# VectorE and SyncE in program order, merged branches split during the last gate block, and the next input without GpSimd, in a two-layer hybrid backbone

## The chip, the cores and the metric

The kernel runs on one core of one Trainium2 chip. The metric is the time of one execution on the device, in microseconds (us); three executions of the kernel before took 2442.62, 2447.07 and 2448.18 us, median 2447.07.

## The reference

Two layers, 512 tokens (256 context, 256 latent), width 2048, everything in fp32. In short, for each layer:

```python
mod = silu(c) @ w_ada[l] + b_ada[l]            # shift, scale, gate; the same of c_ctx
h   = rms_norm(x, norm_g[l]) * (1 + scale) + shift
proj = h @ w_in[l]                             # 2048 -> 12288
y_f = (fourier_mix(f_x) * silu(f_g)) @ w_up_fourier
y_p = (pool_mix(p_x)    * silu(p_g)) @ w_up_pool
# retention, 8 heads of 128: q, k rotated by position (latent tokens only),
# scores with exponential decays in both directions, plus the state of the context
o   = head_rms(o_f + flip(o_b));  y_r = (o * silu(r_g)) @ w_up_ret
g   = sigmoid(proj[:, 6144:])                  # three gates of 2048
x   = x + gate * ((g0 * y_f + g1 * y_p + g2 * y_r) @ w_out)
# ctx gets the same in layer 0; in layer 1 the context gives only k and v
return rms_norm(x, final_norm_g)
```

## The kernel before, in words

**Weights.** Every weight matrix is streamed in chunks of 256 rows by 512 columns (`raw`, 512 KB, four buffers, loaded by SyncE, L196). An fp32 product is made of three products of a rounded high part and the rest, so each chunk is split: ScalarE copies it to the rounded high part `whi` (L206), VectorE subtracts that from `raw` and gives the low part `wlo` (L207). `whi` and `wlo` have three buffers each. TensorE then runs the chunk's products (`mm3`, L151 to L153: two matmuls with `whi`, one with `wlo`). `stream` (L241 to L264) walks over all 512 chunks: it splits the chunk two ahead, loads the one four ahead and runs the products of the present one. So `whi` of a chunk can be written only when TensorE has ended the chunk three before. A chunk is 24 or more products in layer 0 (512 tokens) and mostly 12 in layer 1 (256 tokens).

**Small work.** Between the products stand rotations, decays, scores, norms, transposes. They wait in a queue, `mix` (class Steps, L162 to L182): each entry has a `gap` in modelled microseconds, and `mix.passed` pops entries as products are emitted. A popped entry writes its instructions into the program at that place, for all engines it uses.

**Background.** Gates and modulations of the layers are matrix-vector products on VectorE: units of one `bgraw` load (512 KB, two buffers, on SyncE) and four products with `bga` (L466, L468). `stream` pops a unit behind five of every eight chunks.

**Order.** TensorE runs in the order in which the program text emits its instructions. In the kernel before, the instructions of VectorE, ScalarE, GpSimd and SyncE are put in order by a scheduler; TensorE's are not. Each engine runs its own list strictly in order, and an instruction that waits holds up all behind it.

**Names.** `rope_a` (GpSimd, L597) and `rope_b` (VectorE, L604, L605) rotate q and k; `heads_T` transposes them (L684). `decays_a` makes decay tables (VectorE L708, L709, then three exponentials on ScalarE L710 to L712), `decays_b` finishes them on GpSimd, `scores` multiplies q and k (L732) and weighs the result (VectorE L734), `attend` applies it (L744, L747), `squares` (GpSimd L754, then a split) and `norm_a` (a sum on TensorE L761, a root on ScalarE L762) and `norm_b` (VectorE reciprocal L766, product L767) are the head norm. The generic split of an activation is L431 (ScalarE, high part) and L432 (VectorE, low part). `gated` multiplies by SiLU (L614), SiLU itself is L572. `projected` (L1011 to L1022) adds the residual and, after a row's last piece, takes its sum, a root on ScalarE (L1021) and a reciprocal on VectorE (L1022). `scaled` (GpSimd, L1085) and `next_h` (ScalarE, L1092) make the next layer's input from the transposed rows.

## Time and profile before

| | |
|---|---|
| three executions | 2442.62, 2447.07, 2448.18 us |
| the profiled execution | 2445.55 us, span 2443.8 us |
| TensorE busy | 2392.4 us, 98% |
| VectorE busy | 1320.6 us, 54% |
| ScalarE busy | 870.4 us, 36% |
| GpSimd busy | 240.3 us, 10% |
| mean DMA rate | 162 GB/s |

TensorE is the engine that is nearly always busy, so what counts is where it is not, or where its clock is lower. A matmul's record ends later than the next begins, so busy time is a union of records. In the stretches below, PEclk is the granted clock as a share of 2.4 GHz; 0.5 is 1.2 GHz. Of an engine's idle time the trace names what ended it.

### The profile page before, as it was taken

How to read it: one execution, taken by the hardware profiler on the slowest of the kernel's cores; microseconds unless marked ns; L12 is line 12 of the kernel's file. 1: busy time of each engine (PE TensorE's matmuls, PEld its weight loads, DVE VectorE, ACT ScalarE, POOL GpSimd, SP SyncE). 2: the span in 40 equal slices, each digit the busy share in tenths (PEclk: the TensorE clock that was granted, in tenths of full speed). 3: DMA queues.
4: the chain of work that ended last, by engine and by line, in shares of the span. 5: the costliest groups of instructions: out<-in, count | busy, mean ns of one | idle time of the engine just before them, and what ended most of it. 6: DMA issues, size and time to landing. Idle time of an engine off the chain costs nothing.

```text
span 2443.8 us, 28705 instructions
## 1 busy us (share of the span) xinstructions
PE 2392.4 (98%) x11288; PEld 1967.8 (81%) x11288; DVE 1320.6 (54%) x1656; ACT 870.4 (36%) x1180; POOL 240.3 (10%) x246
## 2 busy tenths in 40 slices
PE   6999999999999999999999999999999999999998
PEld 3678788778888888888888888878889888888886
DVE  4437657768256258644457432653527544545555
ACT  5222332342222232222222322563426444444444
POOL 0000200200000001110011210230302000110100
PEclk9999999999999999999999999999999999999999
DMA  9955424346345336545466343443335666676664
GB/s 338 348 170 173 138 78 148 92 136 213 115 144 187 93 119 210 156 128 169 130 202 215 112 129 112 147 150 103 100 90 146 211 191 180 181 216 183 189 204 146
DMA packets 226471, 396.58 MB, mean 162 GB/s; under 512 B 14032, under 2 KB 55376, under 8 KB 226336
## 3 DMA queue, kind: packets, MB, share of 16 engines
q1 hardware_dynamic: 221088, 379.74, 50.8%
q0 software_dynamic: 5248, 15.01, 2.1%
q8 instruction: 88, 1.44, 0.2%
q14 instruction: 47, 0.39, 0.1%
HBM read 392.60 MB, written 2.10 MB: 162 GB/s over the span
## 4 chain that ended last, share of the span: by engine, by line
PE 81%; issue 8%; DMA 5%; DVE 4%; POOL 1%; ACT 1%; SPq 0%; DVEq 0%; POOLq 0%; ACTq 0%
PE acc L151 25%; PE acc L152 25%; PE acc L153 25%; DVE bga L468 2%; DMA wa<-in_w_ada_dram 2%; DMA bgraw<-in_w_ada_dram 1%; DVE wlo L207 1%; PE mx L323 1%; PE mx L744 1%; PE mx L732 1%; PE mx L747 1%; POOL g L1085 1%; PE mx L701 0%; DMA raw<-in_w_out_dram 0%; PE mx L889 0%
## 5 line engine op out<-in xcount | busy, mean ns | idle before, releaser
L207 DVE TENSOR_TENSOR wlo<-raw,whi 128x1024 fp32r<-128x1024 f32 (+1 forms) x504 | 624.6, 1240 | 824.5 <-ACT whi L206 824.0
L206 ACT ACTIVATE whi<-raw 128x1024 fp32r<-128x1024 f32 (+1 forms) x504 | 529.2, 1050 | 1153.4 <-PE acc L153 553.5
L151 PE MATMUL acc<-whi,hm 128*128 128x512 f32 x1568 | 621.9, 397 | 0.7 <-ACT g L577 0.7
L152 PE MATMUL acc<-wlo,hm 128*128 128x512 f32 x1568 | 611.7, 390 | 2.2 <-DVE wlo L207 2.2
L153 PE MATMUL acc<-whi,hm 128*128 128x512 f32 x1568 | 611.7, 390 | 0.0
L151 PE MATMUL acc<-hm,whi 128*128 128x512 f32 (+1 forms) x1232 | 461.1, 374 | 0.7 <-ACT whi L206 0.7
L153 PE MATMUL acc<-hm,wlo 128*128 128x512 f32 (+1 forms) x1232 | 453.0, 368 | 1.0 <-DVE wlo L207 1.0
L152 PE MATMUL acc<-hm,whi 128*128 128x512 f32 (+1 forms) x1232 | 452.7, 367 | 0.0
L152 PEld LDWEIGHTS acc<-wlo,hm 128*128 128x128 f32 x1568 | 295.1, 188 | 62.7 <-DVE wlo L207 4.1
L153 PEld LDWEIGHTS acc<-whi,hm 128*128 128x128 f32 x1568 | 294.7, 188 | 62.3
L151 PEld LDWEIGHTS acc<-whi,hm 128*128 128x128 f32 x1568 | 295.0, 188 | 61.2 <-ACT g L577 1.1
L468 DVE SCALAR_TENSOR_TENSOR bga<-bgraw,sc,bga 128x512 f32<-128x512 f32 x420 | 311.8, 789 | 53.1 <-DMA bgraw<-in_w_ada_dram 51.5
L151 PEld LDWEIGHTS acc<-hm,whi 128*128 128x128 f32 x1232 | 232.6, 189 | 42.4 <-ACT whi L206 2.2
L153 PEld LDWEIGHTS acc<-hm,wlo 128*128 128x128 f32 x1232 | 232.4, 189 | 40.5 <-DVE wlo L207 2.2
L152 PEld LDWEIGHTS acc<-hm,whi 128*128 128x128 f32 x1232 | 232.6, 189 | 39.4 <-issue 1.4
L852 POOL TENSOR_TENSOR g<-g,g 128x512 f32<-128x512 f32 x32 | 52.7, 1673 | 726.5 <-DVE g L848 726.5
L151 PE MATMUL acc<-g,whi 128*128 128x512 f32 x256 | 99.7, 390 | 0.0
L152 PE MATMUL acc<-g,whi 128*128 128x512 f32 x256 | 99.6, 389 | 0.0
L153 PE MATMUL acc<-g,wlo 128*128 128x512 f32 x256 | 99.6, 389 | 0.0
L597 POOL TENSOR_TENSOR g<-g,g 128x256 f32<-128x256 f32 x32 | 29.6, 954 | 332.4 <-ACT g L577 332.4
L151 PEld LDWEIGHTS acc<-g,whi 128*128 128x128 f32 x256 | 48.1, 188 | 10.1
L152 PEld LDWEIGHTS acc<-g,whi 128*128 128x128 f32 x256 | 48.1, 188 | 10.0
(213 smaller groups left out, 1888.4 us busy)
## 6 DMA issues: line engine op xcount, KB each, us to landing
raw<-in_w_in_dram SPq DMA_DIRECT2D x368, 512.0 KB, 3.7
bgraw<-in_w_ada_dram SPq DMA_DIRECT2D x128, 512.0 KB, 4.3
raw<-in_w_out_dram SPq DMA_DIRECT2D x72, 512.0 KB, 3.6
wa<-in_w_ada_dram SPq DMA_DIRECT2D x128, 256.0 KB, 6.0
raw<-in_w_up_ret_dram SPq DMA_DIRECT2D x32, 512.0 KB, 3.8
raw<-in_w_up_fourier_dram SPq DMA_DIRECT2D x16, 512.0 KB, 3.7
raw<-in_w_up_pool_dram SPq DMA_DIRECT2D x16, 512.0 KB, 4.4
w<-in_w_in_dram SPq DMA_DIRECT2D x8, 512.0 KB, 6.6
```

The source lines that it names most:

```text
L151: T.matmul(ps, ah, bh, start=first, stop=False)
L152: T.matmul(ps, ah, bl, start=False, stop=False)
L153: at["product"] = T.matmul(ps, al, bh, start=False, stop=last)
L206: S.activation(hi[:, :, 0:w], raw[:, :, 0:w], AF.Copy)
L207: V.tensor_tensor(lo[:, :, 0:w], raw[:, :, 0:w], hi[:, :, 0:w].bitcast(F32), op=ALU.subtract)
L323: T.matmul(ps[32 * g4:32 * g4 + 32, 0:2 * n * P], sc32[:, kt, :], wa[gi, kt // rows][:, kt % rows, :, :].rearrange("p i c -> p (i c)"), st ...
L468: V.scalar_tensor_tensor(accs[ci, v], raw[:, kk, :], s, accs[ci, v], op0=ALU.mult, op1=ALU.add)
L597: G.tensor_tensor(rv[:, :, :, x, :], pv[:, :, :, 1 - x, :], sv[:, :, x, :].unsqueeze(1).to_broadcast([P, 4, 2, 32]), op=ALU.mult)
L732: T.matmul(ps[:, jt * SEQ:(jt + 1) * SEQ], self.kT[hh][:, k0:k0 + P], qs, start=True, stop=True)
L744: T.matmul(o, self.v[2 * s + jt][:, c], at[:, jt * SEQ:(jt + 1) * SEQ], start=jt == 0, stop=jt == 1 and s == 0)
L747: T.matmul(o, self.st[d][:, c], qd[:, d * SEQ:(d + 1) * SEQ], start=False, stop=d == 1)
L852: G.tensor_tensor(merged[d][:, 0:ntok], merged[d][:, 0:ntok], o[:, 0:ntok], op=ALU.add)
```

## The change

1. `stream` of all blocks runs with VectorE and SyncE in the order of the program text too, from the first block to the end of the program. ScalarE and GpSimd are still put in order by the scheduler.
2. Chunks of blocks whose split weights are kept (the last block) are split one chunk earlier.
3. Background units are popped only when the queue `mix` has fewer than two entries, behind three of every four chunks.
4. The small work is queued in larger pieces with other gaps: transposes of two heads at once, both states at once, the scores of a head together with the product of the one before, windows and pooled pieces in pairs. In layer 1 k is transposed for its two latent tiles instead of all four.
5. The merged branches are split as they are finished in the last gate block, or in pairs just before the output projection needs them, instead of all sixteen at its start (layer 0); in layer 1 one entry transposes and splits a whole piece.
6. The next layer's input: the scaling moves from GpSimd to VectorE and takes the modulation with it; ScalarE adds the shift while rounding to the high part, VectorE subtracts for the low part.
7. Half of the last output DMAs are issued by ScalarE.

Line numbers shift: L432, L614, L766 become L434, L616, L766; L1020, L1022 become L1028, L1030; L572 becomes L574.

```diff
@@ -258,9 +258,11 @@
         yield
         for i in range(n):
             prepare(i + 2)
+            if i + 3 < n and chunks[i + 3][0].keep:
+                prepare(i + 3)
             ahead(i + 4)
             chunks[i][0].products(chunks[i][1], parts.pop(i))
-            if i > 5 and i % 8 in (1, 3, 5, 6, 7) and bg:
+            if i > 5 and len(mix.q) < 2 and i % 4 and bg:
                 bg.popleft()()
 
 
...
@@ -635,14 +637,14 @@
                 self.k[t] = evac(ps)
                 if t == 3:
                     for t2 in (2, 3):
-                        mix.append(lambda t2=t2: rope_a(self.k, t2), gap=0.8, after=2.0)
-                    mix.append(lambda: self.decayed(0), gap=1.6)
+                        mix.append(lambda t2=t2: rope_a(self.k, t2), gap=1.6, after=2.0)
+                    for d in range(2):
+                        mix.append(lambda d=d: self.decayed(d), gap=1.6)
                     for t2 in (2, 3):
                         mix.append(lambda t2=t2: rope_b(self.k, t2), gap=1.0)
-                    mix.append(lambda: (self.state(0), self.decayed(1)), gap=1.6)
-                    for hh in range(4):
-                        mix.append(lambda hh=hh: self.heads_T(self.k, (0, 1, 2, 3), self.kT, hh))
-                    mix.append(lambda: self.state(1))
+                    mix.append(lambda: (self.state(0), self.state(1)), gap=3.0)
+                    for hh in (0, 2):
+                        mix.append(lambda hh=hh: self.heads_T(self.k, tiles, self.kT, hh), gap=4.0)
                     if last:
                         self.queue_heads()
 
@@ -650,55 +652,53 @@
                 self.q[t] = evac(ps)
                 if t == 3:
                     for t2 in (2, 3):
-                        mix.append(lambda t2=t2: rope_a(self.q, t2), gap=1.2, after=2.0)
+                        mix.append(lambda t2=t2: rope_a(self.q, t2), gap=2.5, after=2.0)
                     for t2 in (2, 3):
                         mix.append(lambda t2=t2: rope_b(self.q, t2), gap=1.0)
-                    for hh in range(4):
-                        mix.append(lambda hh=hh: self.heads_T(self.q, tiles, self.qT, hh))
+                    for hh in (0, 2):
+                        mix.append(lambda hh=hh: self.heads_T(self.q, tiles, self.qT, hh), gap=4.0)
                     if not last:
                         self.queue_heads()
 
             def queue_heads(self):
                 for hh in range(4):
-                    mix.append(lambda hh=hh: self.decays_a(hh), gap=1.0)
+                    mix.append(lambda hh=hh: self.decays_a(hh), gap=2.0)
                 for hh in range(4):
                     mix.append(lambda hh=hh: self.decays_b(hh), gap=1.0)
                 for hh in range(5):
-                    if hh < 4:
-                        mix.append(lambda hh=hh: self.scores(hh))
-                    if hh:
-                        mix.append(lambda hh=hh: self.attend(hh - 1))
+                    mix.append(lambda hh=hh: (self.attend(hh - 1) if hh else None, self.scores(hh) if hh < 4 else None), gap=4.0)
                     if hh > 1:
                         mix.append(lambda hh=hh: self.squares(hh - 2), gap=1.0)
                 mix.append(lambda: self.squares(3), gap=1.0)
                 for hh in range(4):
                     mix.append(lambda hh=hh: self.norm_a(hh))
                 for hh in range(4):
-                    mix.append(lambda hh=hh: self.norm_b(hh))
-
-            def heads_T(self, src, tls, dst, hd):
+                    mix.append(lambda hh=hh: self.norm_b(hh), gap=2.0 if last else 5.0)
+
...
@@ -850,12 +852,24 @@
                         merged[d] = o
                     else:
                         G.tensor_tensor(merged[d][:, 0:ntok], merged[d][:, 0:ntok], o[:, 0:ntok], op=ALU.add)
+                    if final and j == 3:
+                        mix.append(lambda: split_merged(d), gap=0.8, after=0.5)
+
+                def up_before(j=j):
+                    if j == 0:
+                        mix.flush()
 
                 if j == 1 and b == 0:
                     start_at_block(lambda: [bg_gate(l, jj, seqs) for jj in range(4)])
                 fblock(C_MG + b * D + 512 * j, 4, gate_done)
+                if final and j == 3:
+
+                    blocks[-1].during = {k0: lambda d=k0 - 2: (split_merged(d), split_merged(d + 1)) for k0 in range(2, 14, 2)}
                 blocks.append(Block(wview(wname, l, 512 * j, 512), nkt, 512, [("F", i * P, 0, ntok) for i in range(4)],
-                                    lambda kt, t0, n: tuple(x[:, t0:t0 + n] for x in y[kt]), up_done, before=mix.flush if j == 0 else None))
...
@@ -916,10 +930,8 @@
             silu_f[i] = silu(ps)
             if i == 3:
                 for n in range(6):
-                    if n < 4:
-                        mix.append(lambda n=n: positions(n))
-                    if 1 <= n < 5:
-                        mix.append(lambda n=n: channels(n - 1))
+                    if n < 5:
+                        mix.append(lambda n=n: (channels(n - 1) if n else None, positions(n) if n < 4 else None), gap=4.0)
                     if n > 1:
                         mix.append(lambda n=n: mirrored(n - 2), gap=1.0)
...
@@ -993,16 +1004,13 @@
 
         sst, rs = {}, {}
 
-        def split_merged(d):
-            m[d] = split(merged.pop(d), ntok, hmt)
-
         def out_start():
             while bg:
                 bg.popleft()()
-            if not last:
-                mix.flush()
-                for d in range(KT):
-                    split_merged(d)
+
+        def merged_until(kt):
+            while kt not in m:
+                mix.q.popleft()[0]()
 
         def projected(j, t, ps, c0=0, n=512):
             xin = xins.pop((j, t)) if l == 0 else xres[t, j]
...
@@ -1082,15 +1092,18 @@
 
             def scaled(s, kt):
                 xt = xT[s, kt // 2][:, (kt % 2) * SEQ:(kt % 2 + 1) * SEQ]
-                G.tensor_tensor(xt, xt, xT[s][:, 0:SEQ], op=ALU.mult)
+                V.scalar_tensor_tensor(xt, xt, gs[1][:, kt, s:s + 1], xT[s][:, 0:SEQ], op0=ALU.mult, op1=ALU.mult)
                 return xt
 
             def next_h(s, kt):
                 if kt + 1 < KT:
                     xts[s, kt + 1] = scaled(s, kt + 1)
                 xt = xts.pop((s, kt))
-                S.activation(xt, xt, AF.Identity, scale=gs[1][:, kt, s:s + 1], bias=sh[1][:, kt, s:s + 1])
-                h1[kt, s] = split(xt, SEQ, hmt)
+                both = hmt()
+                hh, hl = both[:, 0:SEQ], both[:, SEQ:]
+                S.activation(hh, xt, AF.Identity, bias=sh[1][:, kt, s:s + 1])
+                V.scalar_tensor_tensor(hl, xt, sh[1][:, kt, s:s + 1], hh.bitcast(F32), op0=ALU.add, op1=ALU.subtract)
+                h1[kt, s] = hh, hl
...
@@ -1107,15 +1120,15 @@
                     xres[t, j] = xo
                 if t % 2:
                     s = t // 2
-                    for c2 in range(2):
-                        mix.append(lambda c2=c2: transposed(j, s, c2))
+                    mix.append(lambda: (transposed(j, s, 0), transposed(j, s, 1)), gap=4.0)
                     if j == 3:
                         mix.append(lambda: row_scale(s))
                         for kt in range(KT):
                             mix.append(lambda kt=kt: next_h(s, kt), gap=1.2)
 
             for j in range(3):
-                project(j, (0, 1, 2, 3), done, before=lambda j=j: ((out_start() if j == 0 else None), load_x(j, (0, 1, 2, 3))))
+                project(j, (0, 1, 2, 3), done, before=lambda j=j: ((out_start() if j == 0 else None), load_x(j, (0, 1, 2, 3))),
+                        during={k0: lambda k0=k0: merged_until(k0 + 1) for k0 in range(0, KT, 2)} if j == 0 else None)
             project(3, (2, 3), done, before=lambda: load_x(3, (2, 3)))
             project(3, (0, 1), done, before=lambda: load_x(3, (0, 1)))
 
@@ -1128,13 +1141,14 @@
     for j in range(4):
         bg_mod(1, j)
     run = stream(blocks0 + blocks1)
-    next(run)
-    for t in range(4):
-        halves0[0].v_done(t, v0_acc[t])
-    for i, ps in enumerate(rg_acc):
-        rg_done0(i, ps)
-    for _ in run:
-        pass
+    with tc.manual_schedule(engines={mybir.EngineType.DVE, mybir.EngineType.SP}):
+        next(run)
+        for t in range(4):
+            halves0[0].v_done(t, v0_acc[t])
+        for i, ps in enumerate(rg_acc):
+            rg_done0(i, ps)
+        for _ in run:
+            pass
```

On VectorE at the end of layer 0, the row statistics and the next layer's input (`rs` is a row's scale, `sst` its sum of squares, `hm` the next input, `wlo` the low part of a weight chunk). Before:

```order
L1012 TENSOR_TENSOR g_1799_10975<-g_1799_10975,g_1759_10778 128x512
L432 TENSOR_TENSOR hm_1806_11006<-g_1731_10644,hm_1806_11006 128x256
L207 TENSOR_TENSOR wlo_1808_11010<-raw_1793_10939,whi_1807_11009 128x1024
L1020 TENSOR_REDUCE rs_1801_10980<-sst_1607_9937 128x1
L1011 TENSOR_TENSOR g_1803_10995<-acc_1762_10789,g_1455_8981 128x512
L432 TENSOR_TENSOR hm_1815_11032<-g_1731_10644,hm_1815_11032 128x256
L1022 RECIPROCAL rs_1801_10980<-rs_1801_10980 128x1
L1012 TENSOR_TENSOR g_1803_10995<-g_1803_10995,g_1760_10780 128x512
L432 TENSOR_TENSOR hm_1816_11037<-g_1733_10657,hm_1816_11037 128x256
L432 TENSOR_TENSOR hm_1818_11049<-g_1733_10657,hm_1818_11049 128x256
L207 TENSOR_TENSOR wlo_1820_11053<-raw_1798_10967,whi_1819_11052 128x1024
```

After:

```order
L1028 TENSOR_REDUCE rs_1801_10975<-sst_1607_9939 128x1
L1030 RECIPROCAL rs_1801_10975<-rs_1801_10975 128x1
L1095 SCALAR_TENSOR_TENSOR g_1731_10646<-g_1731_10646,gs1_95,g_1779_10867 128x256
L1105 SCALAR_TENSOR_TENSOR hm_1802_10980<-g_1686_10353,sh1_97,hm_1802_10980 128x256
L1019 TENSOR_TENSOR g_1803_10989<-acc_1762_10791,g_1525_9455 128x512
L1020 TENSOR_TENSOR g_1803_10989<-g_1803_10989,g_1760_10782 128x512
L1028 TENSOR_REDUCE rs_1805_10994<-sst_1610_9951 128x1
L1030 RECIPROCAL rs_1805_10994<-rs_1805_10994 128x1
L1095 SCALAR_TENSOR_TENSOR g_1731_10646<-g_1731_10646,gs1_95,g_1779_10867 128x256
L1105 SCALAR_TENSOR_TENSOR hm_1806_10999<-g_1731_10646,sh1_97,hm_1806_10999 128x256
L207 TENSOR_TENSOR wlo_1808_11003<-raw_1793_10936,whi_1807_11002 128x1024
```

The reciprocal of rs_1805 stood behind two more wlo before; now it stands ahead of wlo_1808, beside four of the three-operand forms.

On ScalarE in layer 1, the roots of the head norms (L762), SiLU (L572, after L574) and the high parts of the weight chunks. Before:

```order
L762 ACT_TABLE_LOAD
L762 ACTIVATE g_2167_13116<-mx_2199_13290,epst_85 128x256
L762 ACTIVATE g_2177_13161<-mx_2200_13306,epst_85 128x256
L206 ACTIVATE whi_2201_13310<-raw_2189_13226 128x1024
L762 ACTIVATE g_2186_13214<-mx_2204_13328,epst_85 128x256
L206 ACTIVATE whi_2206_13348<-raw_2197_13272 128x1024
L762 ACTIVATE g_2193_13250<-mx_2205_13344,epst_85 128x256
L206 ACTIVATE whi_2209_13382<-raw_2203_13314 128x1024
L572 ACT_TABLE_LOAD
L572 ACTIVATE g_2212_13394<-acc_2163_13096 128x256
L572 ACTIVATE g_2212_13394<-acc_2164_13103 128x256
L572 ACTIVATE g_2213_13411<-acc_2168_13118 128x256
```

After:

```order
L206 ACTIVATE whi_2206_13320<-raw_2196_13244 128x1024
L574 ACT_TABLE_LOAD
L574 ACTIVATE g_2209_13332<-acc_2159_13034 128x256
L762 ACT_TABLE_LOAD
L762 ACTIVATE g_2178_13146<-mx_2210_13334,epst_85 128x256
L574 ACT_TABLE_LOAD
L574 ACTIVATE g_2209_13332<-acc_2160_13044 128x256
L574 ACTIVATE g_2211_13351<-acc_2161_13054 128x256
L762 ACT_TABLE_LOAD
L762 ACTIVATE g_2187_13199<-mx_2212_13353,epst_85 128x256
L574 ACT_TABLE_LOAD
L574 ACTIVATE g_2211_13351<-acc_2164_13066 128x256
```

Roots stood together and SiLU together, with two table loads; now they alternate, with five loads between one whi and the next.

On VectorE in the same place, the reciprocals and the splits of gated heads. Before:

```order
L766 RECIPROCAL g_2186_13214<-g_2186_13214 128x256
L207 TENSOR_TENSOR wlo_2210_13383<-raw_2203_13314,whi_2209_13382 128x1024
L767 TENSOR_TENSOR g_2185_13213<-g_2185_13213,g_2186_13214 128x256
L766 RECIPROCAL g_2193_13250<-g_2193_13250 128x256
L207 TENSOR_TENSOR wlo_2215_13423<-raw_2208_13352,whi_2214_13422 128x1024
L767 TENSOR_TENSOR g_2192_13249<-g_2192_13249,g_2193_13250 128x256
L432 TENSOR_TENSOR g_2219_13443<-g_2007_12124,g_2219_13443 128x256
L207 TENSOR_TENSOR wlo_2221_13448<-raw_2211_13386,whi_2220_13447 128x1024
L432 TENSOR_TENSOR g_2223_13459<-g_2014_12151,g_2223_13459 128x256
L432 TENSOR_TENSOR g_2224_13463<-g_2024_12193,g_2224_13463 128x256
L432 TENSOR_TENSOR g_2225_13473<-g_2028_12211,g_2225_13473 128x256
```

After:

```order
L207 TENSOR_TENSOR wlo_2223_13413<-raw_2215_13368,whi_2222_13412 128x1024
L766 RECIPROCAL g_2199_13258<-g_2199_13258 128x256
L767 TENSOR_TENSOR g_2198_13257<-g_2198_13257,g_2199_13258 128x256
L616 TENSOR_TENSOR g_2008_12102<-g_2008_12102,g_2152_12991 128x256
L434 TENSOR_TENSOR g_2225_13433<-g_2008_12102,g_2225_13433 128x256
L207 TENSOR_TENSOR wlo_2227_13437<-raw_2221_13394,whi_2226_13436 128x1024
L616 TENSOR_TENSOR g_2016_12133<-g_2016_12133,g_2152_12991 128x256
L434 TENSOR_TENSOR g_2229_13449<-g_2016_12133,g_2229_13449 128x256
L616 TENSOR_TENSOR g_2022_12162<-g_2022_12162,g_2155_13013 128x256
L434 TENSOR_TENSOR g_2230_13459<-g_2022_12162,g_2230_13459 128x256
L616 TENSOR_TENSOR g_2031_12203<-g_2031_12203,g_2155_13013 128x256
L207 TENSOR_TENSOR wlo_2232_13464<-raw_2224_13416,whi_2231_13463 128x1024
```

Low parts (L434) and products (L616) stood together between wlo; now each L434 stands between two products, one by one, and the wlo behind them.

## Rows read from the trace of the kernel before

**Rows 1.** page, section 1: busy us (share of the span) and instructions of each engine.

```profile
PE 2392.4 (98%) x11288; PEld 1967.8 (81%) x11288; DVE 1320.6 (54%) x1656; ACT 870.4 (36%) x1180; POOL 240.3 (10%) x246
```

**Rows 2.** 50 us stretches after 155 us: busy time of each engine, PEclk, DMA share, GB/s.

```profile
250.00:300.00 50.00, 45.32 (x201) 37.38 (x200) 33.44 (x44) 15.91 (x25) 13.95 (x15) 0.93 0.44 132
400.00:450.00 50.00, 45.46 (x207) 37.07 (x205) 46.40 (x58) 18.75 (x28) 16.12 (x14) 0.99 0.53 162
450.00:500.00 50.00, 47.67 (x202) 39.12 (x202) 31.77 (x42) 16.22 (x29) 6.00 (x6) 0.94 0.31 94
500.00:550.00 50.00, 47.85 (x215) 38.10 (x214) 28.82 (x31) 20.22 (x24) 2.04 (x3) 1.00 0.45 134
1550.00:1600.00 50.00, 48.67 (x221) 39.23 (x221) 37.09 (x51) 36.75 (x67) 18.78 (x20) 1.00 0.61 188
1600.00:1650.00 50.00, 48.36 (x218) 39.32 (x218) 25.64 (x33) 25.97 (x50) 17.64 (x20) 1.00 0.41 125
```

**Rows 3.** waits of TensorE: us in total, times, longest.

```profile
PE mx L732 <- DVE g L734: 5.9, 1, 5.9
PE mx L684 <- DVE g L605: 5.0, 3, 4.6
```

**Rows 4.** timeline of VectorE: start, duration, instruction.

```profile
253.11 4.05 DVE L468 SCALAR_TENSOR_TENSOR bga<-bgraw,sc,bga 128x512 f32<-128x512 f32 x6
257.08 1.28 DVE L604 TENSOR_TENSOR g<-g,g 128x512 f32<-128x512 f32 x2
```

**Rows 5.** groups by line and form, GpSimd and TensorE: busy us, mean ns, idle before.

```profile
L1085 POOL TENSOR_TENSOR g<-g,g 128x256 f32<-128x256 f32 x32 | 31.0, 1006 | 86.0 <-ACT g L1080 86.0
...
L684 PE MATMUL mx<-ident,g 128*128 128x128 f32 x112 | 18.6, 277 | 5.2 <-DVE g L605 5.0
```

**Rows 6.** groups by line and form, VectorE.

```profile
L207 DVE TENSOR_TENSOR wlo<-raw,whi 128x1024 fp32r<-128x1024 f32 x496 | 621.5, 1253 | 817.7 <-ACT whi L206 817.2
L468 DVE SCALAR_TENSOR_TENSOR bga<-bgraw,sc,bga 128x512 f32<-128x512 f32 x420 | 311.8, 789 | 53.1 <-DMA bgraw<-in_w_ada_dram 51.5
...
L766 DVE RECIPROCAL g<-g 128x256 f32<-128x256 f32 x8 | 13.7, 1733 | 0.6 <-ACT g L762 0.6
...
L432 DVE TENSOR_TENSOR g<-g,g 128x256 fp32r<-128x256 f32 x24 | 11.3, 484 | 15.4 <-ACT g L431 15.4
...
L614 DVE TENSOR_TENSOR g<-g,g 128x256 f32<-128x256 f32 x8 | 4.7, 627 | 0.0
...
L767 DVE TENSOR_TENSOR g<-g,g 128x256 f32<-128x256 f32 x8 | 3.1, 400 | 0.0
...
L976 DVE SCALAR_TENSOR_TENSOR g<-mx,vec,g 128x256 f32<-128x256 f32 x4 | 1.9, 482 | 3.6 <-PE mx L973 3.6
```

**Rows 7.** stretches at the start and in layer 1, columns as in Rows 2.

```profile
0.00:100.00 100.00, 79.42 (x428) 47.95 (x432) 48.18 (x142) 39.92 (x77) 1.42 (x6) 0.98 1.06 343
...
1850.00:1900.00 50.00, 50.00 (x336) 46.68 (x335) 39.94 (x49) 30.84 (x53) 16.57 (x21) 1.00 0.52 150
1900.00:1950.00 50.00, 50.00 (x223) 41.39 (x222) 24.25 (x23) 23.94 (x25) 0.57 (x1) 1.00 0.69 207
```

**Rows 8.** timeline of ScalarE at two places.

```profile
1590.58 0.29 ACT L1021 ACTIVATE rs<-rs,epst 128x1 f32<-128x1 f32 x1
...
1876.69 1.04 ACT L206 ACTIVATE whi<-raw 128x1024 fp32r<-128x1024 f32 x1
1877.75 1.28 ACT L762 ACT_TABLE_LOAD   x1
1879.05 0.47 ACT L762 ACTIVATE g<-mx,epst 128x256 f32<-128x256 f32 x1
```

**Rows 9.** groups by line and form, ScalarE.

```profile
L431 ACT ACTIVATE g<-g 128x256 fp32r<-128x256 f32 x24 | 9.5, 420 | 2.8 <-DVE g L976 2.0 <-POOL g L754 0.8
...
L572 ACT ACTIVATE g<-acc 128x256 f32<-128x256 f32 x16 | 4.8, 389 | 0.0
```

**Rows 10.** page, section 6: loads of the background, KB each, median us to landing.

```profile
bgraw<-in_w_ada_dram SPq DMA_DIRECT2D x128, 512.0 KB, 4.3
```

More of the change, by code (lines that the diff above doesn't have):

```diff
@@ L250, in prepare @@
         def prepare(i):
-            if i < n:
+            if i < n and i not in parts:
                 parts[i] = chunks[i][0].split(chunks[i][1], raws.pop(i))
@@ L676, in queue_heads, with heads_T @@
                 for hh in range(4):
[L677 to L679 removed]
+                    mix.append(lambda hh=hh: self.norm_b(hh), gap=2.0 if last else 5.0)
+            def heads_T(self, src, tls, dst, h0):
                 n = len(tls) * P
[L682 to L686 removed]
+                for hd in (h0, h0 + 1):
+                    pt = mx()
+                    for i, t in enumerate(tls):
+                        T.transpose(pt[:, i * P:(i + 1) * P], src[t][:, hd * P:(hd + 1) * P], ident)
+                    dst[hd] = g()
+                    S.copy(dst[hd][:, 0:n], pt[:, 0:n])
             def decayed(self, d):
[L689 removed]
+                self.kd[d] = []
                 for t in range(2):
@@ L700, in state @@
                     for t in range(2):
-                        T.matmul(ps[:, c], self.kd[t][:, c], self.v[t][:, c], start=t == 0, stop=t == 1)
+                        T.matmul(ps[:, c], self.kd[d][t][:, c], self.v[t][:, c], start=t == 0, stop=t == 1)
                 self.st[d] = evac(ps)
@@ L797, in layer, with merged_T @@
         merged, m = {}, {}
-        def merged_T(j, c2):
-            pt = mx()
-            for i in range(2):
-                for t in tiles:
-                    c = (2 * c2 + i) * P
-                    T.transpose(pt[:, (2 * i + t - 2) * P:(2 * i + t - 1) * P], merged[t, j][:, c:c + P], ident)
-            for i in range(2):
-                m[4 * j + 2 * c2 + i] = split(pt[:, i * SEQ:(i + 1) * SEQ], SEQ, hmt)
+        def merged_T(j):
+            pts = []
+            for c2 in range(2):
+                pt = mx()
+                for i in range(2):
+                    for t in tiles:
+                        c = (2 * c2 + i) * P
+                        T.transpose(pt[:, (2 * i + t - 2) * P:(2 * i + t - 1) * P], merged[t, j][:, c:c + P], ident)
+                pts.append(pt)
+            for d in range(4):
+                m[4 * j + d] = split(pts[d // 2][:, (d % 2) * SEQ:(d % 2 + 1) * SEQ], SEQ, hmt)
         def token_branch(b, wname, nkt, y, first, final):
@@ L856, in branch, with split_merged @@
                 fblock(C_MG + b * D + 512 * j, 4, gate_done)
+                if final and j == 3:
+                    blocks[-1].during = {k0: lambda d=k0 - 2: (split_merged(d), split_merged(d + 1)) for k0 in range(2, 14, 2)}
                 blocks.append(Block(wview(wname, l, 512 * j, 512), nkt, 512, [("F", i * P, 0, ntok) for i in range(4)],
-                                    lambda kt, t0, n: tuple(x[:, t0:t0 + n] for x in y[kt]), up_done, before=mix.flush if j == 0 else None))
+                                    lambda kt, t0, n: tuple(x[:, t0:t0 + n] for x in y[kt]), up_done, before=up_before))
+        def split_merged(d):
+            m[d] = split(merged.pop(d), ntok, hmt)
         branch(2, "w_up_ret", 8, y_r, True)
@@ L981, in pg_done @@
             if i == 3:
-                for n in range(5):
-                    if n < 4:
-                        mix.append(lambda n=n: windows(n))
-                    if n:
-                        mix.append(lambda n=n: pooled(n - 1))
+                for n in range(0, 4, 2):
+                    mix.append(lambda n=n: windows(n))
+                    mix.append(lambda n=n: windows(n + 1))
+                    mix.append(lambda n=n: (pooled(n), pooled(n + 1)), gap=3.0)
         tblock(C_PX, tiles, px_done)
@@ L1043, in done @@
                     for i, (xo, o, n) in enumerate(xg[t]):
+                        rows = out[0, (t - 2) * P:(t - 1) * P, o:o + n]
                         if i % 2:
                             S.activation(xo, xo, AF.Copy, scale=rs[t])
+                            nc.scalar.dma_start(out=rows, in_=xo)
                         else:
                             V.tensor_scalar(xo, xo, rs[t], None, op0=ALU.mult)
-                        nc.sync.dma_start(out=out[0, (t - 2) * P:(t - 1) * P, o:o + n], in_=xo)
+                            nc.sync.dma_start(out=rows, in_=xo)
             project(0, tiles, done, before=lambda: (out_start(), final_gains()), during={6: mix.flush})
@@ L1109, in done @@
                     s = t // 2
-                    for c2 in range(2):
-                        mix.append(lambda c2=c2: transposed(j, s, c2))
+                    mix.append(lambda: (transposed(j, s, 0), transposed(j, s, 1)), gap=4.0)
                     if j == 3:
```

14 lines of the change are left out of this document (4 added, 10 removed).

## The prediction

> **What bounds the kernel now.** I read the page's busy times first, then the waits of TensorE, then 50 us stretches, and last the timelines of VectorE and ScalarE. TensorE is busy for 2392.4 of 2443.8 us [rows 1], so the time is TensorE's own work plus the places where it is held up. From 155 us on (what lies before is not touched) the stretches with idle time are few: 250:300, 400:450, 450:500, 500:550, 1550:1600 and 1600:1650 [rows 2]. Their idle time is 4.68 + 4.54 + 2.33 + 2.15 + 1.33 + 1.64 = 16.7 us. Two granted less than the full clock, 0.93 and 0.94, and 400:450 lost 0.01: (0.07 + 0.06 + 0.01) x 50 = 7.0 us at 1.2 instead of 2.4 GHz, each time behind a long wait. Those long waits are on VectorE [rows 3]: 5.9 us for a decayed score (L734) and 4.6 for the rotated k (L605). VectorE was not short of time there; its order was at fault: six background products stand ahead of the rotation at 253 us [rows 4]. So what can be won is small and countable, and everything hangs on whether the new order makes waits elsewhere.
>
> **What goes.** In the new order the rotation and the decayed scores stand where TensorE's program has them, and background work is popped only while the small-work queue is nearly empty. I count 16.0 of the 16.7 us of idle time as gone (not every short wait is VectorE's) and the 7.0 us of slow clock with them. The last layer's k is transposed for two tiles instead of four: 16 transposes of 18.6 / 112 = 0.17 us [rows 5], 2.7 us. The 32 products that leave GpSimd, 31.0 us [rows 5], are off TensorE's path; they become 32 of VectorE's three-operand form at 0.48 [rows 6], 15.4 us, in place of nothing, while ScalarE loses 32 of 0.4 us. Splitting the merged branches earlier costs and wins nothing, since the cover, a full TensorE, is there in both. Gains: 16.0 + 7.0 + 2.7 = 25.7 us.
>
> **What comes.** VectorE now works strictly in the order of the program text, ScalarE does not. Between one chunk's low part (wlo) and the next stands whatever small work the text has there, and if that work waits for ScalarE, all later wlo wait too. TensorE needs wlo of a chunk two chunks later, 5.4 us after the split is due: a chunk in layer 1 is 12 products, 12 x 50/223 = 2.7 us [rows 7], and it can begin two products (0.45 us) before it needs wlo. ScalarE's whi of a chunk can start only when TensorE has left the chunk three before it, as there are three buffers. A wlo that stands behind something which in turn stands behind the *next* whi on ScalarE is therefore late by construction.
>
> - *Row statistics at the end of layer 0 (about 1565 us).* wlo_1808 stands behind the reciprocal of rs_1805. Its root stands on ScalarE behind two later whi, the second of which waits for TensorE's end of the chunk that comes just before the one needing wlo_1808. From there: whi 1.04 and root 0.29 [rows 8], reciprocal about 0.16 (estimate, like the small forms beside it), two three-operand forms 2 x 0.48, wlo 1.25 [rows 6], together 3.7, less 0.45: 3.3 us at least, 5.6 with the backlog that I add up for VectorE ahead of it; I take 4.5. The next wlo has six of these forms ahead: 6 x 0.48 + 1.25 - 2.7 = 1.4, the one after it four, 0.4. Sum 6.3. The other pair of rows, two blocks earlier, has the same knot with a lead of two chunks: 1.5 (0 to 2).
> - *Rotations and decayed scores.* In layer 1 the rotated q is issued one step ahead of its transposes, with two VectorE products per tile ahead of them (two take 1.28 [rows 4]). Four places of 0.5 to 1.5, sum 3.5 (0 to 5).
> - *Decays of the last heads (about 1835 us).* Exponentials and SiLU alternate on ScalarE; four table loads of 1.28 stand ahead of a whi that then comes late, and the decayed score that TensorE wants is queued behind its wlo: 4 x 1.30 less the lead that is left, 4.0 (1 to 4.5).
> - *Head norms, SiLU and their splits (about 1860 to 1890 us).* Roots and SiLU alternate: five table loads between two whi, 5 x 1.30 + 4 x 0.39 + 2 x 0.47 = 9.0 us [rows 8, 9], of which three chunks and the lead hide all but 2.0. Then two reciprocals and two products stand ahead of one wlo, 2 x 1.73 + 2 x 0.40 + 1.25 = 5.5 [rows 6] against 2.7, so 2.8, beside 0.6 and 1.7 for the wlo before and behind it. Then four wlo stand behind low parts whose high parts ScalarE makes only after the next whi: 1.04 + 2 x 0.42 + 0.48 + 0.63 + 1.25 = 4.2 [rows 6, 8, 9], less 2.7 and 0.45: 1.1, twice, and 1.5 for the last. Sum 10.7, of which I take 10.5 (0 to 14). Before, the same stretch has no idle time [rows 7].
>
> New waits: 6.3 + 1.5 + 3.5 + 4.0 + 10.5 = 25.8 us. Waits of 4.6 and 5.9 us each brought 3.4 us of lost clock in [rows 2]; two of the new ones are as long, 6.8 us; in the third place VectorE, not TensorE, sets the pace, so nothing is added. Together 32.6 us (0 to 45).
>
> Against the table loads the Trainium skill has a harsher rule: by ScalarE: Activation LUTs, section What ACT_TABLE_LOAD costs, each switch is 1283 ns and a drain of about 1380 more. Here a load follows a whi by 0.02 us, and the next activation follows the load by 0.02 [rows 8]: the trace disagrees, a switch costs 1.30. By the page the five loads would hold TensorE another 7 us.
>
> **Sum.** 32.6 - 25.7 = +6.9 us on the profiled execution's 2445.55 us, so 2452.5. The median of the runs is 1.5 above that execution: 2454.
>
> **Background in layer 1.** Of 128 loads of 512 KB, 32 now fall into chunks of 2.7 us there, three in every four. Four weight chunks and three of these in 10.9 us are 7 x 0.524 / 10.9 = 337 GB/s; the stretch moves 207 now, the start has 343 [rows 7]. So it fits, barely. VectorE's background products can come to wait for a landing (4.3 us now [rows 10]); the wlo behind them have a lead. I take 0, with an upper end of 11 groups x 1.0 = 11 us if that lead is used up. The page DMA: Bandwidth & Descriptors of the Trainium skill (section Specifications) puts a core's limit at about 358 GB/s; no run here shows more than 343 in such a window.
>
> **Rivals.**
> 1. *Chains overlap more than their durations say (faster).* The place is the head norms and row statistics. Durations count each instruction whole, but neighbours on one engine overlap: six background products take 4.05 us in [rows 4], 0.68 each, where one alone counts 0.79 [rows 6]. If half of each chain is hidden, so that wlo comes within the 0.45 us, the new waits are 13 and the clock falls once: 13 + 3.4 - 25.7 = -9.3 on 2447.07, 2438. It decides where a chain from TensorE's chunk end to wlo is under 3.15 us. Against it: the high parts stand behind the next whi whatever their length.
> 2. *No new wait reaches TensorE (faster).* 2447.07 - 25.7 = 2421. Before, VectorE's and ScalarE's idle shares cover everything from 1850 to 1900 [rows 7]; but that was in an order made free.
> 3. *Background loads starve VectorE in layer 1 (slower by more).* The lead of the wlo is used up and every group of three waits 1.0: +6.9 + 11 + 1.5 on 2445.55, 2465. For it: 337 of the 343 GB/s that any window shows; against it: VectorE is busy only 24 of 50 us there [rows 7].
> 4. *The change does not remove the old waits:* the rotation at 255 us stands in order but its GpSimd half is late, so half of the gain stays away: 2454 + 12 = 2466.
>
> **How the numbers follow.** Forecast 0.45, rival 1 0.22, rival 2 0.12, rival 3 0.13, rival 4 0.08. About 0.2% (4.9 us) can be told from no change. The forecast's own spread, 2444 to 2464, lies for 0.18 within that and for 0.27 above; so faster 0.34, same 0.18, slower 0.48. The range leaves out rival 2's lower part and the top of what rivals 3 and 4 reach: 2428 to 2468.
>
> **What would show it.** Right: no wait over 1 us before 500 us and a full clock there; waits of TensorE on wlo of 3 us and more near 1565, near 1835 on the decayed score, and a row of waits of 1 to 3 us from 1860 to 1890; more table loads. Wrong: stretches of 50.00 busy at those places, or VectorE waiting for background loads between 1900 and 2030.

## The result, and the profile after

The changed kernel takes 2462.01 us (median of four runs, 2461.76 to 2467.35), the kernel before 2445.86: a ratio of 1.0074, 95% interval 1.0062 to 1.0086. Slower by 16 us, inside the range, more than twice as far from no change as the 2454 that was forecast. The profiled execution took 2462.08 us, span 2460.3.

The page's busy times answer to [rows 1]: TensorE has the same work and 16.5 us more of span.

```profile
PE 2394.5 (97%) x11272; PEld 1969.9 (80%) x11272; DVE 1320.3 (54%) x1688; ACT 867.3 (35%) x1154; POOL 199.1 (8%) x214
```

The waits of TensorE (line waited for, us in total, times, longest) answer to [rows 3]. The two long waits of before are gone; new ones have come, first on the low parts of the weights (L207) and on SiLU (L574).

```profile
PE acc L152 <- DVE wlo L207: 11.3, 9, 3.8
PE acc L151 <- ACT g L574: 6.1, 2, 3.2
...
PE mx L744 <- DVE g L734: 2.9, 1, 2.9
PE acc L152 <- DVE g L213: 2.7, 1, 2.7
...
PE acc L151 <- ACT whi L206: 1.9, 1, 1.9
```

The stretches of [rows 2], and where the new waits are (columns as there: TensorE, its weight loads, VectorE, ScalarE, GpSimd, granted clock, DMA share, GB/s):

```profile
250.00:300.00 50.00, 49.35 (x229) 41.27 (x228) 23.53 (x26) 17.76 (x26) 14.36 (x14) 1.00 0.25 74
400.00:450.00 50.00, 49.57 (x228) 41.29 (x227) 23.03 (x24) 19.85 (x30) 16.16 (x17) 1.00 0.16 47
450.00:500.00 50.00, 50.00 (x223) 41.73 (x222) 22.89 (x25) 21.02 (x31) 3.12 (x3) 1.00 0.34 103
500.00:550.00 50.00, 50.00 (x223) 41.39 (x222) 39.64 (x47) 15.74 (x19) 2.05 (x3) 1.00 0.49 161
1550.00:1600.00 50.00, 44.80 (x196) 36.22 (x195) 39.63 (x70) 29.06 (x48) 2.92 (x4) 0.97 0.55 165
...
1700.00:1750.00 50.00, 47.11 (x207) 38.92 (x206) 22.26 (x24) 22.60 (x39) 18.93 (x20) 0.97 0.30 90
...
1850.00:1900.00 50.00, 43.10 (x272) 39.51 (x273) 18.80 (x21) 31.32 (x44) 8.16 (x12) 0.93 0.35 101
1900.00:1950.00 50.00, 44.83 (x187) 35.31 (x186) 38.28 (x50) 22.36 (x28) 3.10 (x5) 0.97 0.73 235
1950.00:2000.00 50.00, 50.00 (x222) 41.34 (x222) 41.26 (x48) 21.97 (x24) 0.00 (x0) 1.00 0.89 311
```

Up to 550 us TensorE is all but full and its clock whole; of 13.7 us of idle time in these four stretches 1.1 is left. In the next four 5.2, 2.9, 6.9 and 5.2 us are idle, and the clock is 0.93 to 0.97. The last, with the background of layer 1, is full. The time at which the n-th weight chunk is split shows where it was won and lost (us against the kernel before, from the two traces; "free" and "mixed" are experiments below):

| chunk | us before | after | free | mixed |
|---|---|---|---|---|
| 130 | 912 | -22.9 | -20.8 | -21.3 |
| 180 | 1189 | -18.9 | -1.5 | -17.3 |
| 250 | 1560 | -18.3 | -1.6 | -16.7 |
| 264 | 1605 | -13.4 | -5.1 | -20.3 |
| 285 | 1709 | -15.9 | -8.0 | -23.2 |
| 300 | 1794 | -6.2 | -7.3 | -22.4 |
| 326 | 1900 | +5.6 | +2.1 | -10.2 |
| 334 | 1922 | +12.3 | +2.2 | -10.1 |
| 503 | 2401 | +15.6 | +2.0 | -10.3 |

So 18 us are won in layer 0, and 34 lost behind it.

The knot at the row statistics, as VectorE's timeline shows it (start, duration, instruction, idle time before it):

```profile
1574.36 0.16 DVE L1028 TENSOR_REDUCE rs<-sst 128x1 f32<-128x4 f32 x1 [0.79 <-ACT g L1025]
1575.49 0.16 DVE L1030 RECIPROCAL rs<-rs 128x1 f32<-128x1 f32 x1 [0.97 <-ACT rs L1029]
1575.57 0.47 DVE L1095 SCALAR_TENSOR_TENSOR g<-g,gs,g 128x256 f32<-128x256 f32 x1
1575.95 0.48 DVE L1105 SCALAR_TENSOR_TENSOR hm<-g,sh,hm 128x256 fp32r<-128x256 f32 x1
1576.34 1.22 DVE L207 TENSOR_TENSOR wlo<-raw,whi 128x1024 fp32r<-128x1024 f32 x1
```

and ScalarE's:

```profile
1573.60 0.63 ACT L1025 ACTIVATE g<-g 128x512 f32<-128x512 f32 x1 [0.99 <-DVE g L1020]
...
1574.23 1.04 ACT L206 ACTIVATE whi<-raw 128x1024 fp32r<-128x1024 f32 x1
1575.17 0.28 ACT L1029 ACTIVATE rs<-rs,epst 128x1 f32<-128x1 f32 x1
```

The reciprocal at 1575.49 waits 0.97 for the root, the root stands behind the whi of 1574.23, and the wlo comes last, at 1576.34. From that whi's start to the wlo's end are 3.3 us (1577.56 - 1574.23), and TensorE, whose last product ahead of the wait began at 1573.45, waited 3.8.

The alternating tables on ScalarE answer to [rows 8]:

```profile
1886.34 1.06 ACT L206 ACTIVATE whi<-raw 128x1024 fp32r<-128x1024 f32 x1
1887.41 1.28 ACT L574 ACT_TABLE_LOAD   x1
...
1889.11 1.28 ACT L762 ACT_TABLE_LOAD   x1
...
1890.90 1.28 ACT L574 ACT_TABLE_LOAD   x1
...
1892.87 1.28 ACT L762 ACT_TABLE_LOAD   x1
...
1894.65 1.28 ACT L574 ACT_TABLE_LOAD   x1
...
1896.23 1.05 ACT L206 ACTIVATE whi<-raw 128x1024 fp32r<-128x1024 f32 x1
```

From the end of one whi to the start of the next are 8.8 us (1896.23 - 1887.40), five loads of 1.28 among them; 9.0 had been worked out. In all there are 36 loads, against 30 before.

### The profile page after: what moved, and what is told of

The parts are those of the page before. It is cut to its first block, busy times and chain, and to the rows that moved or that the text cites. A ratio compares the mean times of both kernels' runs of the same rounds, so it can differ in the third digit from the quotient of the medians.

```text
span 2460.3 us, 28703 instructions
## 1 busy us (share of the span) xinstructions
PE 2394.5 (97%) x11272; PEld 1969.9 (80%) x11272; DVE 1320.3 (54%) x1688; ACT 867.3 (35%) x1154; POOL 199.1 (8%) x214
## 5 line engine op out<-in xcount | busy, mean ns | idle before, releaser
L207 DVE TENSOR_TENSOR wlo<-raw,whi 128x1024 fp32r<-128x1024 f32 (+1 forms) x504 | 620.6, 1233 | 848.1 <-ACT whi L206 847.4
L152 PE MATMUL acc<-wlo,hm 128*128 128x512 f32 x1568 | 613.7, 391 | 10.5 <-DVE wlo L207 10.4
L470 DVE SCALAR_TENSOR_TENSOR bga<-bgraw,sc,bga 128x512 f32<-128x512 f32 x420 | 298.6, 762 | 3.1 <-DMA bgraw<-in_w_ada_dram 2.0
L854 POOL TENSOR_TENSOR g<-g,g 128x512 f32<-128x512 f32 x32 | 43.7, 1393 | 704.7 <-DVE g L850 704.7
L153 PEld LDWEIGHTS acc<-g,wlo 128*128 128x128 f32 x256 | 48.0, 188 | 10.0
L151 PEld LDWEIGHTS acc<-g,whi 128*128 128x128 f32 x256 | 48.1, 188 | 9.9
```

Of the source, the lines that this page charges most:

```text
L151: T.matmul(ps, ah, bh, start=first, stop=False)
L152: T.matmul(ps, ah, bl, start=False, stop=False)
L153: at["product"] = T.matmul(ps, al, bh, start=False, stop=last)
L207: V.tensor_tensor(lo[:, :, 0:w], raw[:, :, 0:w], hi[:, :, 0:w].bitcast(F32), op=ALU.subtract)
L470: V.scalar_tensor_tensor(accs[ci, v], raw[:, kk, :], s, accs[ci, v], op0=ALU.mult, op1=ALU.add)
L854: G.tensor_tensor(merged[d][:, 0:ntok], merged[d][:, 0:ntok], o[:, 0:ntok], op=ALU.add)
```

## The experiments

**Is it the order, or the rest of the change?** Two halves of the change apart. First the changed kernel without its strict order:

```diff
-    with tc.manual_schedule(engines={mybir.EngineType.DVE, mybir.EngineType.SP}):
-        next(run)
+    next(run)
...
```

> The changed kernel, but VectorE and SyncE are put in order by the scheduler again (TensorE alone follows the text); queue, gaps and splits as changed. Theory 1 (the strict order of VectorE makes the new waits): the waits on wlo at 1573 us (3.9), on the decayed score at 1717 (2.9) and the row at 1905 to 1922 (5.6 together) go, the two waits behind table loads at 1848 and 1852 (6.1) and 1895 (1.9) stay, since the table loads are the same 36; time 2440 to 2452, with some of the old waits of 250 to 500 us back. Rival (the new gaps and larger pieces make the waits, the order does not): 2457 to 2465, the waits in the same places.

Measured: 2444.88 us (2443.32 to 2446.93, 11 runs), ratio 1.000 (0.9991 to 1.0009). Then the kernel before with only the strict order added, the same lines the other way round:

> The kernel before, with nothing but VectorE and SyncE set to the order of the text. Theory 1: the two long waits of before at 255 and 446 us shrink, but the same kind of waits as in the changed kernel come at the row statistics near 1570 and from 1700 to 1920; 2450 to 2475. Rival (the gaps): 2425 to 2440, since the order alone only wins.

Measured: 2495.84 us, ratio 1.0203 (1.0189 to 1.0217), above what either theory gave. Stages of these two, columns as above, first the free one:

```profile
150.00:1450.00 1300.00, 1287.08 (x5755) 1062.09 (x5754) 738.76 (x900) 370.96 (x467) 122.08 (x116) 0.99 0.48 147
1450.00:1800.00 350.00, 350.00 (x1610) 291.44 (x1609) 166.77 (x216) 137.70 (x209) 31.43 (x36) 1.00 0.39 119
1800.00:1950.00 150.00, 142.94 (x824) 126.63 (x823) 83.80 (x92) 80.95 (x108) 22.10 (x26) 0.98 0.50 151
```

and the one with the old queue in strict order:

```profile
150.00:1450.00 1300.00, 1275.88 (x5684) 1048.38 (x5683) 681.97 (x825) 365.94 (x456) 110.40 (x116) 0.99 0.43 132
1450.00:1800.00 350.00, 335.12 (x1524) 275.41 (x1523) 166.03 (x188) 147.21 (x242) 63.83 (x68) 0.99 0.38 115
```

The strict order costs 17.1 us with the new queue (2462.01 - 2444.88) and 50 with the old one (2495.84 - 2445.69). With the new queue and no strict order, the waits at 1573, 1717, 1763 and from 1905 on are gone (1450:1800 has no idle time), those behind table loads stay, as theory 1 had it. And the old long waits are gone here too: by chunk 130 this version is 20.8 us ahead of the kernel before. The old queue in strict order is 10.5 us behind there, with 24.1 us of 150:1450 idle. Strict order alone does take the wait at 255 us away and brings the one on the decayed score down to 2.4, but it makes others on wlo, of up to 5.7. So the rest of the change removes the old waits without the strict order, and the strict order alone wins nothing.

It is not one thing. Between 300 and 500 us the free version has no background product at all, so none stands near the decayed score of 446 us any longer. At 255 us five of them still stand ahead of the rotation, where six stood [rows 4], and VectorE begins it at the same time:

```profile
253.78 3.39 DVE L470 SCALAR_TENSOR_TENSOR bga<-bgraw,sc,bga 128x512 f32<-128x512 f32 x5
257.09 1.28 DVE L606 TENSOR_TENSOR g<-g,g 128x512 f32<-128x512 f32 x2
```

There it is TensorE that comes later: 12 more products stand ahead of its transposes (the second state among them), the first of which starts at 258.44 instead of 255.22, and the wait is 1.6 in place of 4.6. The rule for background units, the gaps and the larger pieces were not tested one by one. Why the free order gives its lead back between chunks 130 and 180 the waits of TensorE show:

```profile
PE acc L152 <- DVE wlo L207: 4.6, 1, 4.6
PE acc L151 <- DVE g L968: 4.6, 1, 4.6
```

There VectorE had background units ahead of a wlo and an evacuation, waiting for their loads (3.0 and 2.7 us of idle time for `bgraw` in its timeline). Two waits of 4.6, and 6.8 us at 1.2 GHz behind each.

**Strict in layer 0 only.**

```diff
+            if i == 236:
+                yield
...
+        next(run)
+    for _ in run:
+        pass
```

> The changed kernel with VectorE and SyncE in the order of the text only up to chunk 236 of 512 (before the last parts of layer 0's output projection, about 1470 us); from there the scheduler orders them. Theory 1: the 23 us won before 550 us stay, of the 45 us lost behind 1545 us only those behind table loads stay (about 12); 2428 to 2440, faster than both. Rival: 2455 to 2465.

Measured: 2450.21 us, ratio 1.0018 (1.0009 to 1.0027): neither theory's number. (The 45 us that the expectation names as lost behind 1545 are 34 by the table.) Behind the border all is as theory 1 said (1450:1800 has no idle time), but new waits stand ahead of it:

```profile
PE acc L151 <- DVE g L852: 7.7, 3, 4.6
PE mx L1081 <- DVE g L1022: 4.1, 2, 3.1
PE acc L152 <- DVE wlo L207: 1.4, 2, 0.8
```

The scheduler drew the 32 background units of layer 1 (one load and two products each), which the text has at chunks 336 to 385, forward to 1330 to 1442 us, and VectorE waited for their loads in front of L852 and L1022. So this was tested with the stretch that holds them strict as well:

```diff
+            if i in (236, 334, 390):
+                yield
...
+    next(run)
+    with tc.manual_schedule(engines=strict):
+        next(run)
+    for _ in run:
```

> The changed kernel with VectorE and SyncE in the order of the text up to chunk 236 and from 334 to 390 (where the background of layer 1 stands), and put in order by the scheduler in between and after. If what cost the version with only the first stretch its gain was the 32 background units that the scheduler drew forward to 1374 to 1440 us, its waits there (13 us and 5 of slow clock) go: 2427 to 2434, faster than the kernel before. Rival (any border between the two kinds of order costs that): 2445 to 2452.

Measured: 2430.72 us, ratio 0.9942 (0.9929 to 0.9955), faster than both kernels, as expected; no wait stands at a border, so a border by itself costs nothing that can be seen.

```profile
150.00:1450.00 1300.00, 1297.32 (x5826) 1071.27 (x5826) 697.98 (x841) 376.11 (x472) 111.40 (x116) 1.00 0.43 135
1450.00:1800.00 350.00, 350.00 (x1606) 291.41 (x1605) 166.08 (x216) 136.82 (x208) 31.48 (x36) 1.00 0.40 121
1800.00:1950.00 150.00, 143.32 (x812) 127.14 (x811) 97.20 (x109) 82.22 (x110) 22.12 (x26) 0.95 0.58 178
```

**ScalarE strict as well.** `Activation` added to the strict engines.

> The changed kernel with ScalarE in the order of the text as well. Theory 2 (the knots: a low part waits for a high part that stands behind the next whi): the wait at 1573 falls from 3.9 to about 1, the five waits of 1905 to 1922 (5.6) to 2 or less; 2450 to 2457, table loads the same 36 and their waits unchanged. Rival (VectorE simply has too much to do there): 2460 to 2464, the waits as they were.

Measured: 2469.04 us, ratio 1.0096 (1.0082 to 1.0109). Theory 2's remedy fails: near 1576 TensorE now waits 3.1 for a whi and 0.8 for its wlo, and others grow, as the decayed score's from 2.9 to 4.5. In the text, too, other activations stand ahead of whi, and now ScalarE can pass none of them: ahead of that whi it sits idle for 2.6 and 1.9 us until VectorE has a row's last product (L1020).

**The knots one by one.** The row statistics as queue entries:

```diff
-                V.reciprocal(r, r)
-                rs[t] = r
...
+                if last:
+                    total()
+                    V.reciprocal(r, r)
+                else:
+                    mix.append(total, gap=0.5, after=2.0)
...
+                        mix.append(lambda: [V.reciprocal(rs[2 * s + i], rs[2 * s + i]) for i in range(2)], gap=1.0, after=2.0)
```

> The changed kernel, in which the row sums, roots and reciprocals at the end of layer 0 are queued as small work (sum and root as one entry, the reciprocals as a later one), instead of being written out with the last piece of a row. Theory 2 (knot: the reciprocal waits for a root that stands behind two whi): the wait on wlo near 1573 us falls from 3.9 to under 1 with its 1.7 of slow clock, and 2454 to 2458 in all. Rival (too much work on VectorE there: four products of 0.48 and four of 0.69 between two wlo): it stays above 2.5 and the time within 2 of 2462.

Measured: 2459.71 us, ratio 1.0062 (1.0049 to 1.0075). The wait at 1574 falls from 3.8 to 1.1 and the clock stays whole behind it, so the knot is what made it. Yet only 2.3 us come back, short of the 4 to 8 expected. In the trace 1.4, 0.6 and 0.9 us of new waits follow at 1589, 1596 and 1622, on things that this entry pushed back in the queue, and behind the same wait of 2.9 at 1718 TensorE runs at 1.2 GHz for 6.8 us instead of 3.4. The profiled execution, 2463.61, is the slowest of the five, so these waits and the median can't be set off to the tenth. The split of gated heads two heads behind their product:

```diff
-                mix.append(parts, gap=0.8, after=0)
+                waiting.append(parts)
+                made[0] += 1
+                while len(waiting) > (0 if not last or made[0] == HEADS else 2):
+                    mix.append(waiting.popleft(), gap=0.8, after=0)
```

> The changed kernel, in which the split of a gated head in layer 1 is queued two heads behind its product, so that VectorE no longer waits for ScalarE between one and the other. Theory 2 (low parts waiting for high parts): the waits from 1909 to 1922 (1.6, 1.1, 0.6, 1.1) fall to under 1.5 together; 2457 to 2460. Rival (VectorE has just too much to do between the wlo): they stay at 4, 2461 to 2463.

Measured: 2461.02 us, ratio 1.0064 (1.0051 to 1.0077). The waits on wlo between 1897 and 1930 us fall from 5.9 to 1.9 in all, as the knot says:

```profile
PE acc L152 <- DVE wlo L207: 1.9, 4, 0.9
```

but the time moves by 1.0 only, within the spread of the two: in 1800:1950 the granted clock is 0.94 instead of 0.97 (17.1 us at 1.2 GHz instead of 10.2, behind about the same waits on SiLU and whi), and the wait at the end of the program (L213) grows from 2.7 to 3.4. Last, SiLU of the retention gate in layer 1 left out:

```diff
-            silu_r[hd] = silu(ps)
+            silu_r[hd] = silu(ps, AF.Copy if last else AF.Silu)
```

> The changed kernel, with the SiLU of the retention gate in layer 1 left out (a copy in its place, same instruction count and size), so that ScalarE needs 27 table loads instead of 36. Theory 3 (alternating tables hold back whi and the accumulators): the waits at 1848 and 1852 (6.5) and at 1895 and 1897 (3.0) go to under 1 each, with 3.4 to 5.1 of slow clock: 2447 to 2452. Rival (the waits come from VectorE's strict order, which keeps the decays late): those at 1848 and 1852 stay above 2, 2457 to 2461.

Measured: 2451.72 us, 10.3 less, ratio 1.0025 (1.0015 to 1.0035). It is within theory 3's time; the waits on SiLU between 1830 and 1930 fall from 6.1 to 1.4, not below 1, and 1.0 on a decayed score is new. The table loads are 27 instead of 36.

```profile
PE acc L152 <- DVE wlo L207: 3.8, 4, 1.5
PE acc L151 <- ACT g L574: 1.4, 1, 1.4
```

**A version from what was learned.** The mixed order, with the exponentials and the roots of layer 1 queued in groups, so that tables change more seldom (29 loads instead of 36). All four heads' decays and roots at once:

> The mixed order, and in layer 1 the decay tables of four heads are queued as one entry, and the roots of four heads as one, so that ScalarE needs 29 table loads instead of 36. If the loads cause the waits of the mixed order at 1832, 1833 and 1878 to 1882 us (7.8, with 5.1 of slow clock), most of that goes: 2419 to 2424. Rival (the roots in one go make TensorE wait for the fourth accumulator, and the decays in one go hold VectorE): 2428 to 2432.

Measured: 2428.85 us, ratio 0.9933 (0.9919 to 0.9947). The rival has it: the loads are gone, but four decays in one go hold up a whi by 2.1 us at 1704 and by 1.5 at 1837. Decays in two pairs:

> As the one before, but the decay tables in two pairs. Same 29 loads: 2419 to 2424; if VectorE's four decays in one go cost something, this one is 1 to 3 faster than it.

Measured: 2425.14 us, ratio 0.9919 (0.9905 to 0.9932), 3.7 less, more than the 1 to 3 expected; TensorE waits 2.3 us for the fourth root's accumulator. Roots in two pairs as well:

```diff
+                    for h2 in (0, 2):
+                        mix.append(lambda h2=h2: [self.decays_a(h2 + hh) for hh in range(2)], gap=2.0)
...
+                    for h2 in (0, 2):
+                        mix.append(lambda h2=h2: [self.norm_a(h2 + hh) for hh in range(2)], gap=1.5)
```

> As the one before, but the roots in two pairs as well. Same 29 loads: 2419 to 2424; if TensorE waits for the fourth root's accumulator, this one is 0.5 to 2 faster than it.

Measured: 2423.45 us (2422.74 to 2425.04), ratio 0.9912 (0.9899 to 0.9926): 21.7 us faster than the kernel before, 38.6 faster than the change. Its longest waits behind 160 us:

```profile
PE acc L151 <- ACT g L576: 2.0, 1, 2.0
PE mx L694 <- DVE g L609: 1.1, 2, 0.6
PE mx L513 <- ACT g L508: 0.9, 1, 0.9
```

## Why the prediction was right, and where not

The waits of this list are counted from the start of one product to the start of the next, less the usual step (0.22 us, in layer 1 also 0.12). That gives up to 0.3 us more than the views, in which a wait begins where a product's record ends.

- **What bounds it, and the direction:** right. TensorE's work is the same, and the balance is waits won against waits made, on wlo, behind roots and table loads. All places named (1565, 1835, 1860 to 1890, with a shift of up to 30 us) had them.
- **What goes:** forecast 25.7. Measured 18.3 by chunk 250, beside the waits that before had at 1586 to 1621, 3.8 in all; the 16 transposes can't be told apart in the table. The size was nearly right. The prediction gave two reasons in one breath: "the rotation and the decayed scores stand where TensorE's program has them, and background work is popped only while the small-work queue is nearly empty". The first was not needed: the version without strict order wins 20.8 us by chunk 130, and strict order alone, with the old queue, loses 10.5. The second fits at 446 us, not at 255. What the strict order does by itself is to keep that lead: the free version loses some 15 us more between 130 and 180, on which nothing stood in the prediction.
- **Row statistics:** forecast 7.8 and 3.4 of clock. Measured at 1546, 1549, 1553 and 1573: 0.9 + 0.3 + 1.5 + 3.9 = 6.6, and a half clock of 3.4 us, which is 1.7 lost. For the wait at 1573 the mechanism is shown by its experiment; the wait at 1553 stayed there.
- **Rotations and decayed scores:** with its clock the term most mis-sized, 3.5 against 3.1 at 1717 and 2.4 at 1763 and 1.7 of clock behind each, 8.9. At 1717 the decays themselves are slow on VectorE (below).
- **Decays of the last heads:** 4.0 forecast; 3.0 + 3.5 and 3.4 of clock came. The wait was not on the decayed score, as written, but on accumulators that SiLU had not emptied. That the table loads make most of it, leaving SiLU out shows.
- **Head norms and splits:** 10.5 forecast; 2.0 + 1.0 + 1.5 + 1.6 + 1.1 + 0.6 + 1.1 = 8.9, and 1.7 of clock.
- **The clock:** 6.8 us forecast, in two places; from 1545 on it was six stretches at 1.2 GHz, 23.9 us long, 11.9 lost. Waits of 2.4 to 3.9 us brought it too, which the prediction had not charged. A wait's length alone does not tell: 2.0 us at 1836 brought 3.4 us at 1.2 GHz in the version before the last and none in the last, and 3.5 us at 1413 brought none with the old queue in strict order. (The "7.0 us at 1.2 instead of 2.4 GHz" of the prediction are time lost; the stretches were 13.7 us long.)
- **The end of the program:** not in the sum. 2.8 on the kept low parts (L213), 1.0 and 0.9 on wlo, 1.0 on a high part, and 1.7 of clock, where before had waits of 3.8. From chunk 334 to the last matmul the offset grows from 12.3 to 15.9.
- **The sum:** by the spans the change is 16.5 us slower, 9.6 more than the 6.9 forecast. Of these the clock makes 5.1, the end of the program 1.9 (5.7 against 3.8), the waits 1.7 (27.5 against 25.8) and the gains 0.9 (24.8 against 25.7, with the transposes at the 2.7 forecast). Among the four terms of waits errors of 1 to 3 us cancelled; the rest all point one way, so the time lies above the forecast and the clock is the term that failed by most. The prediction's own slips (the head norms add up to 10.8, not 10.7; four chunks of 2.7 are 10.8 us, not 10.9) change nothing.
- **Rivals.** Of the 337 GB/s in layer 1 [rows 7, 10], 311 came. (The 343 that the prediction names as the most in any window is a mean over 100 us; 50:100 of the kernel before moves 353.) VectorE did wait for background loads there, a sign that the prediction had set for being wrong: 5.7 us between 1900 and 2100, 3.2 of them before 2030. None of it reached TensorE, and in the whole program these waits are 12.7 us, 57.2 before: rival 3 did not come. Rivals 1 and 2 fell with the waits; rival 4 too, 0.8 us is left at the rotation of 257 us. On table loads the trace went on disagreeing with the page ScalarE: Activation LUTs of the Trainium skill (section What ACT_TABLE_LOAD costs), which adds a drain of about 1380 ns to each switch: here a switch is 1.28 and 0.02 us, with no drain to be seen.

Left open: how much of the 4 us between chunks 130 and 180 that every version with the new queue and strict order there loses is only work moved across the mark; which part of the new queue removed which of the old waits; and why the clock falls behind one wait and not behind another of the same length.

## What to carry to other kernels

An order written by hand is as good as its worst knot: look on each engine for an instruction whose input stands, on another engine, behind the very thing that TensorE frees last. In this kernel it paid to take the scheduler's order in stretches where small work crosses engines, and the text's order where long background work would otherwise be drawn in front. Before crediting an order with a gain, run the other half of the change without it; here the other half had won it, and for the background rule, too, the trace shows that it explains one of two waits. Taking waits away gave back 10.3 us where they came from table loads, but 2.3 of 4.4 (clock included) and 1.0 of 4.0 where one knot among several was undone; new waits and a lower clock took the rest.
